# Row maxima of the 64-row attention heads from 128-row products

## The chip, the cores and the metric

The kernel runs on one core of a Trainium2 chip. The metric is the device time of one execution in microseconds (us); less is better. Before the change the median of three runs is 3290.38 us.

## What is computed

Two layers of a transformer over 512 image tokens and 256 context tokens, 1024 features wide. Each layer is a SwiGLU feed-forward network, a mixer and a second feed-forward network, each with a modulated norm ahead of it. The mixer projects its input, runs four mixers of four heads side by side and projects their outputs back. Cut to what matters here:

```
x  = x + 0.5*mx[2]*swiglu(pre_norm(x, ...))
ux = split_in(pre_norm(x, ...) @ w_in)
ya, yac = swa_mixer(...)        # windowed attention, 4 heads of 64, with a sink
yd, ydc = deltanet_mixer(...)   # gated delta rule, both directions
ym, ymc = mla_mixer(...)        # latent attention, 4 heads of 96 rows (64 + 32 rotary)
yn, ync = na_mixer(...)         # neighbourhood attention, 4 heads of 64, with a bias
x  = x + mx[5]*(concat([ya, yd, ym, yn]) @ w_out)
x  = x + 0.5*mx[8]*swiglu(pre_norm(x, ...))
...
def joint_softmax(*logits):     # local and context scores share one softmax
    p = softmax(concat(logits, axis=-1))
```

In the second layer only the image tokens are needed behind the mixer, so it has no context queries. Everything is float32 in the reference.

## The kernel before

The kernel is traced by a Tile scheduler: the code gives the operations in an order of its own, and the scheduler places them on the engines by its own estimate of their times, so that work of several generators is interleaved on each engine. Tiles of type F32R are single-pass products on TensorE; a float32 value is held as a pair of such tiles, high and low part, and a product takes three terms: high by high, low by high and high by low. Tiles of type F32 go through TensorE in a slower form (the values of the attention, the delta-rule chain, the transposes). Masks and biases are BF16.

The mixer stage of a layer has two generators side by side. `dn_chain` (lines 1193 to 1308) is the recurrence of the delta rule over 24 block steps, a chain of small products on TensorE (names t, mb, sp, op, pt, yt) with work of VectorE, ScalarE and GpSimd between them. `attentions` goes through twelve heads: four windowed ("swa"), four of the neighbourhood ("na"), four latent ("mla"). One step of the attention is traced for each step of the chain; when the chain ends, the rest of the attention follows. For each head and each block of 128 keys, `scores` makes transposed scores in PSUM (lines 687 to 689 for heads of 96 rows, 691 and 692 for heads of 64 rows, the mask on line 710), ScalarE takes the exponential (line 717, tile p), and `values` multiplies p by the values into tile o (lines 735 and 738). The next head's `row_max` runs beside these, up to four steps for each key block; two heads ahead, `load` issues the loads of queries and keys on GpSimd's queue.

`row_max` gives the number that is subtracted ahead of the exponential. For every block of 128 queries, line 637 multiplies the queries by the 256 context keys (tile sc) and line 644 by the image keys that the block sees (tile sl: 256 or 384 columns for a head of 64 rows, 512 for one of 96); lines 649 and 652 add masks and bias as further products into sl. VectorE reduces each with a maximum (lines 638 and 654). The sc and sl banks come from a PSUM ring of two, called r. At the end the maxima are transposed on TensorE (line 673, tile mt) and ScalarE writes them, negated, as one more row below the queries (line 674), where the score products pick them up against a row of ones in kb.

A head of 64 rows is loaded as these operands:

```
qa = [hi; hi] (128 rows)   qb = [lo; -max] (65 rows)
ka = [hi; lo] (128 rows)   kb = [hi; ones] (65 rows)
```

Line 691 multiplies ka by qa over 128 rows and line 692 kb by qb over 65. The row maxima come from `qh, kh = hd["q"][0], hd["k"][1]` (line 632), that is from qa and kb, cut to `Kd` rows: 64 for the swa and na heads, 96 for the mla heads. For the 64-row heads that is high by high alone.

The queues around it: `load_k` issues ka and then kb on GpSimd's queue, and `load_q` qa and then qb behind them. SyncE carries the weights, the stores of the mixers' outputs (yd) and their loads for the output projection (yl, line 1391). ScalarE carries the exponentials and, from the end of the chain on, casts of weights (wh) and of yl (xnhA, xnhC, line 269).

Of the kernel before, what the change touches and what calls it, by code (L numbers as in the profile page):

```python
# [6 lines left out]
F32 = mybir.dt.float32  # L7
# [5 lines left out]
PSUM = bass.MemoryType.PSUM  # L13

D = 1024
# [3 lines left out]
FF = 2816  # L19
# [14 lines left out]
class Net:  # L34
# [30 lines left out]
    def open_xn(self):  # L65
        """the normalised activations; their side of the memory changes with every opening"""
        self.side_x, self.side_o = self.side_o, self.side_x
        self.xnp = self.tc.tile_pool(name="xn", bufs=1, side=self.side_x, reuse_waits="tile")
        p = self.xnp.__enter__()
        self.XNh, self.XNl = {}, {}  # L70
        for q, t in self.T.items():
            self.XNh[q] = p.tile([128, KD, t], F32R, name="xnh" + q)
            self.XNl[q] = p.tile([128, KD, t], F32R, name="xnl" + q)
# [13 lines left out]
    def weights(self, pool, w, sets=None):  # L87
        """pool of the weight tiles. The raw tiles, free early, lie where the pool's successor puts its first tiles"""
        self.wp, self.ww, self.wsets, self.wn = pool, w, sets, -1
        tags = ["wr", "wh", "wl"] if sets is None else ["w%s%d" % (t, n) for n in range(sets) for t in "rhl"]  # L90
        left = self.side_x == "left"
        if sets is None:
            tags = tags if left else tags[1:] + tags[:1]
        else:
            tags = tags if left else tags[3:] + tags[:3]
        for t in tags:
            pool.tile([128, w], F32 if t[1] == "r" else F32R, tag=t, name=t)

    def psum(self, shape=(128, 512), name="pt", ring=None):
        """a PSUM bank of ring p, r or d; of self.rings in turn when none is named"""  # L100
        if ring is None:
            ring = self.rings[self.bank % len(self.rings)]
            self.bank += 1
        return self.ps.tile(list(shape), F32, tag=ring, name=name, bufs=BANKS[ring])

    def aux(self):
        """a ring of the attentions' side work: r, and d as well once the chain is traced"""
        self.auxn += 1
        return self.auxr[self.auxn % len(self.auxr)]

    # ---------------------------------------------------------------- inputs
# [5 lines left out]
    # ------------------------------------------------------- ada modulation  # L117
# [10 lines left out]
    def ada(self, l):  # L128
        """generator: modulation vectors of layer l, in steps of one weight row block.
        The first two vectors of layer 0 come from the tensor engine, the others are summed over the  # L130
        row blocks beside the FFNs, where it has no time to spare, and over the partitions at the end."""
# [15 lines left out]
        for j in range(2 if l == 0 else 0, 9):  # L147
            acc = [self.wa.tile([128, 512], F32, tag="acc", name="adaacc", bufs=AB) for _ in range(4)]
            for k in range(KD):
                for g in range(2):  # L150
                    w = self.wa.tile([128, 512], F32, tag="wa", name="adaw")
                    if l == 0 and j == 2 and k < WB // 2:
                        # no load before the first norm is done: its own come first
                        nc.gpsimd.tensor_copy(w[:, 0:1], self.XNl["A"][:, KD - 1, 0:1].bitcast(F32))
# [33 lines left out]
    def mod_cols(self, l, j):  # L188
        """scale -> g*(1+scale), gate of the sublayer (halved for the FFNs)."""
# [9 lines left out]
    def fill(self, n):  # L199
        """n steps of the work that is done beside the FFNs"""  # L200
# [4 lines left out]
    # ------------------------------------------------------------------ norm  # L205
    def unit(self, u):
        """A: the image's tokens, A0 and A1: halves of them, C: the context's; part, columns and their number"""
# [6 lines left out]
    def sumsq(self, u, m):  # L214
        """add chunk m of X to the running sum of squares."""
# [12 lines left out]
    def rstd_bc(self, ss, nb, dim, ring=None):  # L228
        """1/sqrt(sum(ss)/dim + eps) of every token, on all partitions."""
# [22 lines left out]
    def norm(self, u, i):  # L252
        """XN = X*rstd*g*(1+scale)+shift as an exact high/low pair."""
# [22 lines left out]
    # --------------------------------------------------------------- weights  # L276
    def weight(self, ap, w):
        """load a weight tile of w columns per partition, split into high/low."""
# [15 lines left out]
    # ------------------------------------------------------------------- FFN  # L294
    def ffn(self, l, i, parts, fill=0, save=(), then=None, ns=0):
        """X += gate * swiglu(XN); i-th sublayer's (0 or 2) modulation. then(unit): what follows a unit's last chunk"""
# [62 lines left out]
    # ---------------------------------------------------------------- output  # L359
    def final(self, u):  # L360
        """the final norm of a unit, to the output"""
# [11 lines left out]
def pack(inp):  # L373
# [14 lines left out]
    up = np.stack([np.stack([a[f"ffn{i}_wg"], a[f"ffn{i}_wu"]], 1) for i in (1, 2)], 1)  # L,2,2,D,FF  # L388
    r["wgu"] = c(up.reshape(L, 2, 2, KD, 128, NF, 128).transpose(0, 1, 5, 4, 2, 3, 6)).reshape(L, 2, NF, 128, 2, 1024)
    dn = np.stack([a["ffn1_wd"], a["ffn2_wd"]], 1)  # L,2,FF,D  # L390
# [8 lines left out]
class Mix:  # L399
    """projections of the mixers (kept in DRAM scratch ud) and the three attentions"""  # L400
# [27 lines left out]
    # ---------------------------------------------------------- projections  # L428
# [22 lines left out]
    def store(self, l, ch, parts, perm=False, fn=ACTF.Copy):  # L451
        """project chunk ch and keep it in ud"""
# [7 lines left out]
    def keep(self, ch, rows, w, src):  # L460
        """keep src, {first column: values}, as a high/low pair in hl or mk"""
# [6 lines left out]
        for j, t in enumerate((hi, lo)):  # L468
# [8 lines left out]
            else:  # L477
                # a head's rows: queries hi, hi, lo; keys hi, lo
# [4 lines left out]
    def store_pair(self, l, ch, parts, perm=False, rope=False):  # L483
        """project chunk ch and keep it as a high/low pair"""
# [15 lines left out]
    # ------------------------------------------------------ latent attention  # L500
    def mla_up(self, l, need):
        """normalised latents, their up-projections with the rotary part, to ud"""
# [37 lines left out]
        # shared rotary key: columns 32:64 of chunk 0, its swapped copy in 64:96; kept in rows 64:96  # L540
# [46 lines left out]
    # ------------------------------------------------------------ attention  # L587
    def load_v(self, ch):
        """values of the two heads of a chunk, token-major with a column of ones"""
# [12 lines left out]
    def load_q(self, ch, h, w):  # L602
        """a head of 64 rows as operands [hi; hi] and [lo]: with the keys' [hi; lo] and [hi] two products
        cover the three terms high*high, low*high and high*low"""
# [13 lines left out]
    def load_mla(self, h, w, kb):  # L618
        """a head of 96 rows as high/low pairs"""
# [8 lines left out]
    def row_max(self, hd):  # L628
        """minus the row maxima of the scores, in the row below the queries"""
        nc = self.nc  # L630
        Kd, nq, loc, bias = hd["Kd"], hd["nq"], hd["loc"], hd["bias"]
        qh, kh = hd["q"][0], hd["k"][1]
# [43 lines left out]
    def scores(self, hd, kb):  # L676
        """probabilities of the queries that see key block kb; kb None: the context's queries"""
# [42 lines left out]
    def values(self, hd, kb, pp):  # L720
        """add a key block's share to the unnormalised outputs, token-major; their column 64 sums the probabilities"""
# [3 lines left out]
        if kb == 4:  # L725
            # a product with zeros opens the bank for all blocks of queries
# [14 lines left out]
    def finish(self, hd):  # L741
        """normalise the outputs of a head; store them, feature-major, when both heads of a chunk are done"""
# [23 lines left out]
    def attentions(self, l, need):  # L766
# [5 lines left out]
        def edge(b):  # L772
            # the block on the left is masked where f < p, the one on the right where f > p
# [92 lines left out]
def mix_pack(inp, r):  # L866
# [9 lines left out]
    # rotary halves of the windowed heads: first halves of both axes, then second halves  # L876
# [4 lines left out]
    win = np.stack(chunks, 1)  # L,NCH,D,128  # L881
    r["win"] = c(win.reshape(L, NCH, KD, 128, 128).transpose(0, 1, 3, 2, 4)).reshape(L, NCH, 128, 1024)
    # rotary tables
# [22 lines left out]
    # masks  # L906
# [6 lines left out]
    def ok(qb, kb):  # [q, k]  # L913
# [25 lines left out]
    # latent attention  # L939
# [3 lines left out]
    uq = np.concatenate([uq, uq[:, :, :, 64:][:, :, :, sw]], 3)  # L,256,4,128  # L943
# [6 lines left out]
class DN:  # L950
    """gated delta rule mixer, both directions"""
# [14 lines left out]
    # -------------------------------------------------- projection and conv  # L966
    def dn_tokens(self, l, need, dp, dt):
        """short convolution and silu of k, q, v, token-major"""
# [28 lines left out]
    # -------------------------------------------------------------- gates  # L997
    def dn_gates(self, l, ab, gp, dt):
        """log decay g, beta [128 tok, 6, 8] and their cumulated forms"""
# [11 lines left out]
        # log1p(e) = 2 atanh(e / (2 + e))  # L1011
# [30 lines left out]
        egn = gp.tile([128, 2, 6, 2, 2], F32, name="egn")  # n, m, dir, pair  # L1042
# [7 lines left out]
    # ---------------------------------------------------------- preparation  # L1050
    def dn_prep(self, l, need, tok, ab, late, dp, dt):
        """normalised keys and queries, decays and the inverses of the 32x32 diagonal blocks"""
# [57 lines left out]
        def invert(d):  # L1110
# [11 lines left out]
            # 32x32 diagonal blocks, one block per partition, lower triangular  # L1122
# [29 lines left out]
    # ---------------------------------------------------------------- chain  # L1152
    def dn_chain(self, l, need, tok, prep, pc):
        """chunk-wise maps, state recurrence and outputs of both directions"""
# [18 lines left out]
        def chain(d):  # L1173
            for mi in range(6):
# [74 lines left out]
                # state recurrence and the outputs that depend on it  # L1249
# [42 lines left out]
    def dn_out(self, m, Oa, ng, pc):  # L1292
        """gated norm of a token block, feature-major, to the mixer outputs"""
# [43 lines left out]
class Kern(Net, Mix, DN):  # L1337
# [46 lines left out]
    def second_half(self, l, parts, then):  # L1384
        """output projection of the mixers and the second FFN"""
        nc = self.nc
        def take(k):
            for p in parts:
# [4 lines left out]
                if p == "A" and k >= 6:  # L1393
                    # the neighbourhood heads' blocks of columns, to the order of the tokens
# [16 lines left out]
        # the first output chunks, a mixer at a time in the order that they come  # L1411
# [40 lines left out]
    def mixers(self, l, need):  # L1452
# [13 lines left out]
        with ExitStack() as keep:  # L1466
# [4 lines left out]
            with ExitStack() as sx_st:  # L1471
                # a set of weight tiles after the other: the first lies on the raw tiles of the FFN's weights, which are free early
# [100 lines left out]
```

## Time and profile before

| what | us |
| --- | --- |
| timed runs | 3284.80, 3290.38, 3295.83 |
| median of the runs | 3290.38 |
| span of the profiled execution, first to last instruction | 3284.4 |
| stretch of the swa and na heads' maxima in layer 0 | 898 to 1065 |
| the same in layer 1 | 2615 to 2761 |

The profile has no run time of its own for the profiled execution, only its span; the median of the runs lies 6.0 us above that span. In a row of the timeline the second number is how long the instruction, or the run of like instructions, lasted; starts of successive products on TensorE are closer together than their durations, because products overlap in the array. In the chain of waits each piece is the time by which the end moved on, so that pieces add up to elapsed time. A form such as 64*128 64x256 is a product of 64 rows and 128 columns of weights with a moving operand of 256 columns. fp32r tiles are printed as f32.

### The profile page before, as it was taken

The numbers are of one execution on the slowest core, as the hardware profiler recorded it, in microseconds if no ns is written. First come the engines' busy times: TensorE is split into PE (matmuls) and PEld (weight loads), VectorE is DVE, ScalarE is ACT, GpSimd is POOL, SyncE is SP. The second block draws the span as 40 slices with busy tenths as digits, with TensorE's granted clock in tenths as the row PEclk, the third lists the DMA queues.
The fourth block names the chain that finished last, engine by engine and source line by source line (L and its number), as shares of the span: only waits on it lengthen the run. The fifth ranks groups of instructions, "written<-read, shape, count | busy, mean of one in ns | idle before, by whom it ended". The sixth has DMA issues, their size and how long they took to land.

```text
span 3284.4 us, 48913 instructions
## 1 busy us (share of the span) xinstructions
PE 3162.0 (96%) x19586; PEld 2721.2 (83%) x19586; DVE 1719.3 (52%) x3044; ACT 1069.4 (33%) x1927; POOL 465.6 (14%) x772
## 2 busy tenths in 40 slices
PE   7999999898999999999999999999997899999998
PEld 4888888887778889888889988888886688788887
DVE  5746354736744567766735432322747744353334
ACT  3212212555444423121224312122455343342223
POOL 2201000410323021111102000000311322000001
PEclk9999999998999999999999999999998999899999
DMA  6434232513623353444423221212423612323333
GB/s 246 148 103 140 83 118 81 170 59 119 175 71 81 90 193 114 157 134 136 134 73 117 67 68 58 71 52 66 147 77 113 169 49 70 118 92 98 95 96 107
DMA packets 135396, 357.45 MB, mean 109 GB/s; under 512 B 20000, under 2 KB 33824, under 8 KB 134912
## 3 DMA queue, kind: packets, MB, share of 16 engines
q1 hardware_dynamic: 101056, 255.47, 24.8%
q0 software_dynamic: 34112, 98.85, 10.6%
q8 instruction: 154, 2.52, 0.3%
q14 instruction: 74, 0.61, 0.1%
HBM read 316.89 MB, written 39.65 MB: 109 GB/s over the span
## 4 chain that ended last, share of the span: by engine, by line
PE 58%; DVE 3%; DMA 2%; ACT 1%; issue 1%; POOL 0%; SPq 0%; POOLq 0%; DVEq 0%; ACTq 0%
PE dacc L290 5%; PE dacc L291 5%; PE dacc L292 5%; PE gA L290 4%; PE gA L291 4%; PE uA L290 4%; PE uA L292 4%; PE uA L291 4%; PE gA L292 4%; PE guC L292 3%; PE guC L290 3%; PE guC L291 3%; PE o L738 2%; PE pj L292 1%; PE pj L290 1%
## 5 line engine op out<-in xcount | busy, mean ns | idle before, releaser
L269 ACT CAST wh<-wr 128x1024 fp32r<-128x1024 f32 (+5 forms) x443 | 394.8, 893 | 1235.2 <-PE dacc L291 454.8
L274 DVE TENSOR_TENSOR wl<-wr,wh 128x1024 fp32r<-128x1024 f32 (+5 forms) x443 | 460.6, 1042 | 420.0 <-ACT wh L269 390.4
L290 PE MATMUL dacc<-hh,wh 128*128 128x256 f32 (+1 forms) x1392 | 452.3, 326 | 2.6 <-ACT wh L269 2.3
L292 PE MATMUL dacc<-hh,wl 128*128 128x256 f32 (+1 forms) x1392 | 450.4, 326 | 2.8 <-DVE wl L274 2.8
L291 PE MATMUL dacc<-hl,wh 128*128 128x256 f32 (+1 forms) x1392 | 452.1, 326 | 0.0
L161 DVE SCALAR_TENSOR_TENSOR adaacc<-adaw,silc,adaacc 128x512 f32<-128x512 f32 x448 | 315.0, 747 | 11.4 <-DMA adaw<-ada_w 11.2
L290 PE MATMUL guC<-xnhC,wh 128*128 128x256 f32 x1056 | 300.4, 285 | 1.6 <-ACT xnhC L263 1.6
L291 PE MATMUL guC<-xnlC,wh 128*128 128x256 f32 x1056 | 300.3, 285 | 1.6 <-DVE xnlC L264 1.6
L292 PE MATMUL guC<-xnhC,wl 128*128 128x256 f32 x1056 | 300.2, 284 | 0.5 <-DVE wl L274 0.5
L290 PEld LDWEIGHTS dacc<-hh,wh 128*128 128x128 f32 x1392 | 261.4, 188 | 31.9 <-ACT wh L269 6.1
L290 PE MATMUL gA<-xnhA,wh 128*128 128x512 f32 (+1 forms) x752 | 285.3, 380 | 2.2 <-ACT xnhA L263 2.2
L292 PEld LDWEIGHTS dacc<-hh,wl 128*128 128x128 f32 x1392 | 261.0, 188 | 28.5 <-DVE wl L274 3.9
L290 PE MATMUL uA<-xnhA,wh 128*128 128x512 f32 (+1 forms) x752 | 283.1, 376 | 1.0 <-ACT wh L269 1.0
L292 PE MATMUL gA<-xnhA,wl 128*128 128x512 f32 (+1 forms) x752 | 283.4, 377 | 0.0
L292 PE MATMUL uA<-xnhA,wl 128*128 128x512 f32 (+1 forms) x752 | 282.8, 376 | 0.4 <-DVE wl L274 0.4
L291 PE MATMUL uA<-xnlA,wh 128*128 128x512 f32 (+1 forms) x752 | 283.0, 376 | 0.0
L291 PE MATMUL gA<-xnlA,wh 128*128 128x512 f32 (+1 forms) x752 | 282.9, 378 | 0.0
L291 PEld LDWEIGHTS dacc<-hl,wh 128*128 128x128 f32 x1392 | 261.4, 188 | 24.7
L133 POOL DMA_DIRECT2D adaw<-ada_w x256 | 140.1, 548 | 802.6 <-DVE adaacc L159 484.7
L348 DVE SCALAR_TENSOR_TENSOR xA<-dacc,modG,xA 128x512 f32<-128x512 f32 (+1 forms) x160 | 101.9, 640 | 239.3 <-PE dacc L292 239.3
L290 PEld LDWEIGHTS guC<-xnhC,wh 128*128 128x128 f32 x1056 | 203.1, 192 | 9.3 <-ACT wh L269 5.0
L291 PEld LDWEIGHTS guC<-xnlC,wh 128*128 128x128 f32 x1056 | 203.3, 193 | 4.4 <-DVE xnlC L264 2.0
(350 smaller groups left out, 5955.6 us busy)
## 6 DMA issues: line engine op xcount, KB each, us to landing
wr<-wgu SPq DMA_DIRECT2D x176, 512.0 KB, 3.6
adaw<-ada_w POOLq DMA_DIRECT2D x256, 256.0 KB, 3.2
wr<-wd SPq DMA_DIRECT2D x120, 320.0 KB, 3.0
wr<-wd SPq DMA_DIRECT2D x64, 384.0 KB, 3.1
wr<-win SPq DMA_DIRECT2D x44, 512.0 KB, 3.6
adaw<-ada_w SPq DMA_DIRECT2D x32, 256.0 KB, 5.2
hl<-eh SPq DMA_DIRECT2D x32, 192.0 KB, 3.0
hl<-el SPq DMA_DIRECT2D x24, 192.0 KB, 3.2
```

The lines of the kernel that those rows point to most:

```text
L133: load = lambda q, t, k, c: q.dma_start(out=t, in_=self.I["ada_w"][l, k * 128:(k + 1) * 128, c:c + 512])
L161: nc.vector.scalar_tensor_tensor(out=t, in0=w, scalar=c, in1=t, op0=ALU.mult, op1=ALU.add)
L269: nc.scalar.copy(hi, src)
L274: (nc.vector if leng == "V" else nc.gpsimd).tensor_tensor(lo, src, hi.bitcast(F32), op=ALU.subtract)
L290: nc.tensor.matmul(out, lhsT=wh, rhs=xh, start=start, stop=False)
L291: nc.tensor.matmul(out, lhsT=wh, rhs=xl, start=False, stop=False)
L292: nc.tensor.matmul(out, lhsT=wl, rhs=xh, start=False, stop=stop)
L348: nc.vector.scalar_tensor_tensor(out=x, in0=acc, scalar=gate[:, i, m, r:r + 1], in1=x, op0=ALU.mult, op1=ALU.add)
L738: nc.tensor.matmul(o[:, q0 + q], lhsT=p[:, q * 128:q * 128 + 128], rhs=v(kb), start=False, stop=kb == 3 and q == n // 128 - 1)
```

## The change

`row_max` takes, for heads with `Kd` of 64, all 128 rows: qa = [hi; hi] by ka = [hi; lo] in place of the upper 64 rows of qa by those of kb. The sum over 128 rows is high by high plus high by low. The latent heads keep their 96 rows and kb. No instruction is added or left out. Comments and docstrings are taken out elsewhere, which changes nothing; from here on lines are numbered two higher. The diff, cut to its core:

```diff
     def row_max(self, hd):
-        """minus the row maxima of the scores, in the row below the queries"""
+
         nc = self.nc
         Kd, nq, loc, bias = hd["Kd"], hd["nq"], hd["loc"], hd["bias"]
-        qh, kh = hd["q"][0], hd["k"][1]
+
+        Kd, kh = (128, hd["k"][0]) if Kd == 64 else (Kd, hd["k"][1])
+        qh = hd["q"][0]
         mx = self.tp.tile([128, 6, 2], F32, tag="mx", name="mx", bufs=2)
         for qb in range(nq):
             lq = qh[0:Kd, qb * 128:(qb + 1) * 128]
```

TensorE in layer 1, a neighbourhood head's maxima (L637, L644) among the scores (L691, L692), masks (L649, L710), bias (L652) and values (L738) of the head ahead of it, before:

```order
14197 L710 MATMUL st<-masks,identb 128x256
14198 L637 MATMUL sc<-kb,qa 128x256
14199 L738 MATMUL o<-v,p_25385 128x65 x4
14200 L691 MATMUL st<-qa,ka 128x384
14201 L692 MATMUL st<-qb,kb 128x384
14202 L644 MATMUL sl<-kb,qa 128x256
14203 L649 LDWEIGHTS identb
14204 L649 MATMUL sl<-masks,identb 128x256
```

And the same place after the change, its lines two higher:

```order
14193 L712 MATMUL st<-masks,identb 128x256
14194 L639 MATMUL sc<-ka,qa 128x256
14195 L740 MATMUL o<-v,p_25385 128x65 x4
14196 L693 MATMUL st<-qa,ka 128x384
14197 L694 MATMUL st<-qb,kb 128x384
14198 L646 MATMUL sl<-ka,qa 128x256
14199 L651 LDWEIGHTS identb
14200 L651 MATMUL sl<-masks,identb 128x256
```

Nothing has moved here; the two products of the maxima read ka where they read kb.

ScalarE in layer 0, where the latent heads (exponentials p, maxima mt) meet the output projection's casts (wh from weights, xnhA and xnhC from the loaded outputs yl), before:

```order
600 L674 ACTIVATE qa<-mt 1x512
601 L269 CAST wh<-wr 128x384 x2
602 L674 ACTIVATE qa<-mt 1x256
603 L269 CAST xnhA<-yl 128x512
604 L269 CAST xnhC<-yl 128x256
605 L717 ACTIVATE p_10550<-st 128x512
606 L717 ACTIVATE p_10570<-st 128x512
607 L269 CAST xnhA<-yl 128x512
608 L269 CAST xnhC<-yl 128x256
609 L717 ACTIVATE p_10598<-stc 128x512
610 L717 ACTIVATE p_10620<-st 128x512
```

After:

```order
600 L676 ACTIVATE qa<-mt 1x512
601 L269 CAST wh<-wr 128x384
602 L676 ACTIVATE qa<-mt 1x256
603 L269 CAST wh<-wr 128x384
604 L269 CAST xnhA<-yl 128x512
605 L719 ACTIVATE p_10550<-st 128x512
606 L269 CAST xnhC<-yl 128x256
607 L719 ACTIVATE p_10570<-st 128x512
608 L719 ACTIVATE p_10598<-stc 128x512
609 L269 CAST xnhA<-yl 128x512
610 L269 CAST xnhC<-yl 128x256
611 L719 ACTIVATE p_10620<-st 128x512
```

Three exponentials instead of two stand ahead of the second pair of casts, and one of the maxima's rows ahead of the second weight cast. Elsewhere the engines' orders differ in a few short runs, mostly in the same products of neighbouring work changing places.

## Rows read from the trace of the kernel before

**Rows 1.** The page's first line: the profiled execution.
```profile
span 3284.4 us, 48913 instructions
```

**Rows 2.** Groups by shape on TensorE: form, count | busy us, mean ns | idle before.
```profile
L637 PE MATMUL sc<-kb,qa 64*128 64x256 f32 x80 | 31.6, 396 | 3.3 <-DMA qa<-hl 3.1 <-DVE mx L638 0.2
...
L637 PE MATMUL sc<-kb,qa 96*128 96x256 f32 x40 | 15.7, 408 | 2.0 <-DVE mx L654 1.8 <-ACT v L599 0.2
...
L644 PE MATMUL sl<-kb,qa 64*128 64x384 f32 x32 | 14.1, 441 | 0.1
...
L644 PE MATMUL sl<-kb,qa 64*128 64x256 f32 x32 | 12.3, 385 | 0.2
```

**Rows 3.** Busy time in two stretches: PE, PEld, DVE, ACT, POOL; clock; DMA.
```profile
898.00:1065.00 167.00, 166.07 (x1441) 133.89 (x1440) 79.83 (x216) 72.03 (x184) 51.31 (x97) 1.00 0.35 79
2615.00:2761.00 146.00, 144.92 (x1220) 116.38 (x1221) 63.80 (x163) 61.18 (x157) 45.29 (x89) 0.95 0.30 78
```

**Rows 4.** TensorE's waits, 2615 to 2761 us: us in total, times, longest.
```profile
PE sc L637 <- DMA qa<-hl: 3.1, 1, 3.1
```

**Rows 5.** Timeline of TensorE in layer 1: start, duration, instruction, form.
```profile
2746.50 0.37 PE L691 MATMUL st<-qa,ka 128*128 128x256 f32 x1
2746.70 0.28 PE L692 MATMUL st<-qb,kb 65*128 65x256 f32 x1
...
2747.04 0.38 PE L637 MATMUL sc<-kb,qa 64*128 64x256 f32 x1
2747.35 1.11 PE L738 MATMUL o<-v,p 128*128 128x65 f32 x8
```

**Rows 6.** Chain of waits in the same place: start, us, what.
```profile
2746.75 0.12 PE st L691
...
2746.99 0.13 PE st L710
2747.11 0.31 PE sc L637
2747.42 1.04 PE o L738 x8
2748.46 0.23 PE st L691
...
2748.87 0.31 PE sl L644
2749.18 0.21 PE sl L649
...
2749.67 0.84 PE o L738 x8
```

**Rows 7.** Chain of waits among the latent heads of layer 0.
```profile
1135.62 0.84 PE o L735 x8
1136.46 0.17 PE sc L637
...
1137.80 0.12 PE sc L637
```

**Rows 8.** Timeline of TensorE, layer 1: maxima between chain products.
```profile
2750.66 0.33 PE L1264 MATMUL sp<-S,MT 64*64 64x64 f32 x4
2750.92 0.38 PE L637 MATMUL sc<-kb,qa 64*128 64x256 f32 x1
2751.23 0.33 PE L1264 MATMUL sp<-S,MT 64*64 64x64 f32 x4
```

**Rows 9.** Timeline, layer 1: a chain result and who reads it.
```profile
2662.18 0.69 DVE L1201 TENSOR_TENSOR vk<-vk,t 128x512 f32<-128x512 f32 x1 [0.24 <-PE t L1199]
...
2663.60 1.05 PE L1204 MATMUL t<-vk,tbd 128*128 128x128 f32 x8
```

**Rows 10.** Busy time as in rows 3, behind layer 0's last chain step.
```profile
1100.60:1103.60 3.00, 0.47 (x5) 0.23 (x3) 1.42 (x5) 0.17 (x1) 1.64 (x2) 1.00 0.41 97
1103.60:1118.40 14.80, 12.70 (x49) 9.46 (x49) 8.93 (x20) 6.47 (x13) 0.00 (x0) 0.54 0.62 194
```

## The prediction

> **What bounds the kernel now.** I first asked which engine sets the pace where the changed products stand. The profiled execution spans 3284.4 us [rows 1]; the three timed runs are 3284.80, 3290.38 and 3295.83, so their median lies 6.0 us above that span, and I carry the 6.0 us over. The changed products are those on lines 637 and 644 that run on 64 rows: 80 with 256 columns, and on line 644 32 with 256 and 32 with 384 columns, 144 in all; the 40 on line 637 that run on 96 rows belong to the latent heads and stay as they are [rows 2]. Along TensorE's timeline the 144 lie in two stretches, 898 to 1065 us (layer 0, 80 of them) and 2615 to 2761 us (layer 1, 64). The reader should see in the windows that TensorE is busy for 166.07 of 167.00 us and for 144.92 of 146.00 us there, while VectorE and ScalarE are busy for less than half of each [rows 3]. The one long wait, 3.1 us, is for a load of queries as the second stretch begins [rows 4]. In the chain of waits, followed back from the end, the second stretch is TensorE work laid end to end, and these very products are pieces of it [rows 6]. So TensorE's own sequence is the bound, and the question is what one 64-row product takes out of it, with what it does to its neighbours.
>
> **What a 64-row product costs today.** The timeline shows it. The 128-row L691 of 256 columns starts at 2746.50 and lasts 0.37, but the next product starts at 2746.70, 0.17 us before L691 is over: products overlap. The 64-row L637 starts at 2747.04 and lasts 0.38; the next product starts at 2747.35, only 0.07 us before its end [rows 5]. The next one, now of full height, has to get going anew. The chain of waits has the same as pieces that add up to the elapsed time: 0.31 us for the 64-row L637, 0.31 for the 64-row L644; the eight o products behind L637 take 1.04 us where eight behind a full-height product take 0.84; the mask product behind L644 takes 0.21, and a mask product of the same 256 columns behind a full-height product 0.13 [rows 6]. The two sorts of neighbour differ in nothing but the height of the product ahead.
>
> **What it will cost.** The change removes no instruction and adds none; it doubles the rows of both operands of 144 products. No row of before shows exactly the new product, but two are close. One is L637 itself for the latent heads, with 96 rows and 256 columns, the same kind of tiles, the same PSUM ring and the same reader: its piece is 0.17 us behind o products and 0.12 behind an fp32r product, and o products follow it and its like at 0.84 for eight [rows 7]. The other is L691, all 128 rows of the same ka and qa: 0.12 us for 256 columns behind a transpose, and 0.23 for 384 behind o products [rows 6]. So I take 0.17 behind o and mask products and 0.12 behind the others, which saves 0.14 or 0.19 of the 0.31. The 384-column ones cost 441 ns against 385 ns of busy time [rows 2], that is 56 ns for the further columns, which they will also cost in the new form; I give them the same savings.
>
> Who stands beside them is counted along TensorE's timeline of the two stretches. Ahead of the 144: 54 times an o or a mask product, 54 times another full-height product, 12 times another of the 144, and 24 times a product of the delta-rule chain that itself works on a part of the array. Behind them: 65 times a mask product, 34 times an fp32 product (o, a chain step, a transpose), 11 times an fp32r one, 12 times another of the 144, 22 times a chain product on a part of the array. Beside such partial products I count nothing: L1264 works on 64 by 64, and an L637 between two of them takes 0.31 us from start to start [rows 8]; the new form will still differ from both sides.
>
> The sum: own pieces 54 x 0.14 + 54 x 0.19 = 17.8 us; followers 65 x 0.08 (0.21 less 0.13) + 34 x 0.20 (1.04 less 0.84) + 11 x 0.19 (an fp32r follower, 0.31 less 0.12) = 14.1 us. Together 31.9 us. Bounds: if the new product takes 0.23 everywhere, the dearest ordinary piece of L691, and mask products gain nothing, it is 108 x 0.08 + 45 x 0.20 = 17.6 us; if all 108 save 0.19 and all 110 followers 0.20, it is 42.5 us. A loss from the products themselves I exclude, since every full-height piece of this size in these rows is under 0.31.
>
> **What moves with it.** Row maxima now wait for the load of ka rather than kb; the first score product, which reads both, waits for kb instead. Both loads leave GpSimd's queue together, and the queries leave it last: the only load that TensorE waits for there is that of qa [rows 4]. I cost this at nothing; if a ka load came late, the whole score sequence behind it would have waited for it anyway. No buffer is held longer, because the scores read ka after the maxima do. The order on the engines is almost the same. The larger differences stand where layer 0's latent heads meet the output projection: on ScalarE exponentials there move ahead of casts that wait for loads. I cost it at nothing, between plus and minus 2 us, since on either order TensorE has products queued.
>
> Is the gain passed on? What follows the stretches hangs on TensorE: the chain's steps, the stores of the mixers, and the loads that wait for those stores. The other engines' work stays as it is in stretches that shrink by a tenth, so VectorE's 79.83 of 167.00 us becomes about half. The chain's results lie ready before they are read: in the tightest case inside the stretches once the pipeline has filled, VectorE's L1201 ends at 2662.87 and L1204 reads it at 2663.60, 0.73 us later [rows 9]; it is the shortest of the 8 such pairs of the second stretch, the others have 1.34 us and more. Two shortened products within such a gap take some 0.6 us from it. So nearly all is passed on.
>
> **The rivals.** First, the height does not matter and the 0.31 us has another cause that stays (kb, the ring, the reductions): the time stays at 3290. Weighing against it: the 96-row products on the same line share kb, ring and reader and take 0.12 to 0.17 [rows 7]. The Trainium skill speaks for it, on the page TensorE: Matmul & The Clock Gate: under LDWEIGHTS (loading the stationary operand) the load's time goes by columns and not by the contraction, and the table under Why this matters for your kernels has a lone product of 32 rows take as long as one of 128. By that rule the change saves nothing; the trace agrees in busy time (385 and 396 ns for 64 rows, 408 ns for 96 [rows 2]) but not in when the neighbours start. I give it 6 in 100.
>
> Second, a partial gain: TensorE comes closer to its feeders and half of the 31.9 us goes into new waits for VectorE and ScalarE in the delta-rule chain, 3290.4 - 16 = 3274. For it: the 0.73 us of [rows 9]. Against: most gaps are several times that. 9 in 100.
>
> Third, slower: TensorE outruns the chain so far that it falls idle, and the granted clock falls. Such a place is in the trace, behind the last chain step of layer 0: 3.00 us with 0.47 busy, then 14.80 us at a granted clock of 0.54, close to 1.2 of 2.4 GHz [rows 10]. Its price is about 2.5 us idle and 14.8 x 0.46 = 6.8 us of slow products, 9.3 together. Four such stalls more would take the 31.9 us back; from five it is slower, at 3258 + 46 = 3304. It needs waits of microseconds where the gaps shrink by tenths: 3 in 100.
>
> **How the numbers follow.** The forecast is 3290.4 - 31.9 = 3258 us (span about 3252), with 82 in 100. Its own bounds are 3290.4 - 42.5 = 3248 and 3290.4 - 17.6 = 3273; with some 3 us of scatter, and the partial case mostly taken in, the range is 3245 to 3275. About 0.3%, 10 us, is what a measurement of this kernel can tell from no change, so faster means below 3280: the forecast, and nearly all of the partial case, 0.90. Within 0.3%: the first rival and the rest, 0.07. Slower: 0.03.
>
> **What would show it.** The groups of lines 637 and 644 (two lines lower in the new file) should drop from 385 and 396 ns on average towards 300 to 370, with 128 rows in their shape. The chain of waits should have 0.12 to 0.17 us where 0.31 stands, and eight o products behind them at 0.84. The first stretch should shrink by about 17 us and the second by about 14, with TensorE as busy as now. I am wrong if these pieces stay at 0.31; if they fall and the stretches do not shrink, the waits of TensorE on VectorE and ScalarE must have grown; if the stretches shrink and the end does not, a load or the clock in the tail of the attentions has taken it.

## The result, and the profile after

The changed kernel takes 3254.89 us (median of four runs, 3252.43 to 3255.82) against 3293.11 us for the kernel before beside it (3284.80 to 3299.08): a ratio of 0.9885, with a 95% interval from 0.9866 to 0.9904. It is faster by a little over 1%, 3 us below the forecast of 3258 and inside its range. The lines of the new file stand two higher: L637 is L639, L644 is L646, the scores' L691 is L693, the o products' L738 is L740.

The page's first line, and its row of engines, whose PE was 3162.0 us before:

```profile
span 3252.6 us, 48912 instructions
PE 3129.6 (96%) x19586; PEld 2713.3 (83%) x19586; DVE 1715.9 (53%) x3044; ACT 1069.6 (33%) x1927; POOL 463.6 (14%) x772
```

The span is 31.8 us shorter than in [rows 1], TensorE's busy time 32.4 us. VectorE's, ScalarE's and GpSimd's moved by 3.4 us at most. Groups by shape on TensorE, as in [rows 2] (form, count | busy us, mean ns | idle before):

```profile
L639 PE MATMUL sc<-ka,qa 128*128 128x256 f32 x80 | 30.0, 376 | 0.7 <-DVE mx L640 0.3 <-ACT v L599 0.3 <-ACT yt L764 0.2
...
L646 PE MATMUL sl<-ka,qa 128*128 128x384 f32 x32 | 13.2, 412 | 0.2
...
L646 PE MATMUL sl<-ka,qa 128*128 128x256 f32 x32 | 11.5, 359 | 0.4 <-DVE mx L656 0.3
```

The duration of one product fell by 20 to 29 ns, from 396, 441 and 385. Over 144 products that is 3.4 us, a tenth of the gain. Whoever reads the groups alone would take the change for nearly worthless. The gain stands in the places between the products. The chain of waits in layer 1, at the place of the work that answers to [rows 6] (start, us, what):

```profile
2712.14 0.12 PE st L693
...
2712.37 0.12 PE st L712
2712.50 0.12 PE sc L639
2712.62 0.84 PE o L740 x8
2713.46 0.23 PE st L693
...
2713.87 0.12 PE sl L646
2713.99 0.12 PE sl L651
...
2714.38 0.84 PE o L740 x8
...
2715.71 0.32 PE sc L639
2716.02 0.26 PE sp L1266 x4
```

Line by line against [rows 6]: the maxima product of line 639 has 0.12 us where 0.31 stood, the eight o products behind it 0.84 where 1.04 stood, line 646 has 0.12 for 0.31 and the mask product behind it 0.12 for 0.21. The last two rows are the place of [rows 8], between chain products on 64 by 64, and there the piece is 0.32 us still. TensorE's timeline of the same place (start, duration, instruction, form) answers to [rows 5]:

```profile
2712.26 0.37 PE L639 MATMUL sc<-ka,qa 128*128 128x256 f32 x1
2712.46 1.00 PE L740 MATMUL o<-v,p 128*128 128x65 f32 x8
```

The product itself lasts 0.37 us as against 0.38, but the next one now starts 0.17 us before its end and not 0.07. The weight loads (PEld, the loading of a product's stationary operand) of the same two rows, first before the change, then after:

```profile
2747.04 0.18 PEld L637 LDWEIGHTS sc<-kb,qa 64*128 64x128 f32 x1
2747.35 0.97 PEld L738 LDWEIGHTS o<-v,p 128*128 128x128 f32 x8
```

```profile
2712.22 0.20 PEld L639 LDWEIGHTS sc<-ka,qa 128*128 128x128 f32 x1
2712.34 0.98 PEld L740 LDWEIGHTS o<-v,p 128*128 128x128 f32 x8
```

The load of the o products followed 0.31 us behind that of the 64-row product and follows 0.12 us behind that of the 128-row one. Over the 144 products a load now starts a median of 55 ns behind the start of the product ahead, where it was 203 ns before; the load itself lasts about as long (192 and 183 ns). So the loads, which now run beside the product ahead, stood back until that product was nearly over.

The two stretches of [rows 3], cut at the same work (busy us of PE, PEld, DVE, ACT, POOL; clock; DMA):

```profile
895.00:1045.50 150.50, 149.01 (x1438) 129.67 (x1438) 78.07 (x214) 71.82 (x183) 52.81 (x99) 0.99 0.38 89
2595.00:2725.00 130.00, 129.39 (x1219) 112.81 (x1219) 62.78 (x163) 61.13 (x159) 44.34 (x87) 0.96 0.34 84
```

From first to last maxima product the first stretch went from 166.25 to 150.37 us and the second from 144.89 to 129.75. That is 15.9 and 15.1, together 31.0 of the 31.8 us, and TensorE is as full as before in both.

### The profile page after: what moved, and what is told of

Read it like the earlier page. It is cut to its first block, busy times and chain, and to the rows that moved or that the text cites. A ratio compares the mean times of both kernels' runs of the same rounds, so it can differ in the third digit from the quotient of the medians.

```text
span 3252.6 us, 48912 instructions
## 1 busy us (share of the span) xinstructions
PE 3129.6 (96%) x19586; PEld 2713.3 (83%) x19586; DVE 1715.9 (53%) x3044; ACT 1069.6 (33%) x1927; POOL 463.6 (14%) x772
## 4 chain that ended last, share of the span: by engine, by line
PE 57%; DVE 4%; issue 3%; DMA 2%; ACT 1%; POOL 0%; POOLq 0%; DVEq 0%; SPq 0%; ACTq 0%
PE dacc L290 4%; PE dacc L292 4%; PE dacc L291 4%; PE gA L290 4%; PE gA L291 4%; PE uA L290 4%; PE uA L292 4%; PE uA L291 4%; PE gA L292 4%; PE guC L292 3%; PE guC L290 3%; PE guC L291 3%; PE o L740 2%; PE pj L290 1%; PE pj L292 1%
```

## Experiments

Ratios are to the kernel before, run beside each, whose medians there lay between 3292.4 and 3294.9 us. The diffs are against the changed kernel where nothing else is said.

**The tile or the height.** The change swaps kb for ka as well as 64 rows for 128. This kernel takes the new tile and the old height; its order on every engine is that of the kernel before.

```
-        Kd, kh = (128, hd["k"][0]) if Kd == 64 else (Kd, hd["k"][1])
+        Kd, kh = (64, hd["k"][0]) if Kd == 64 else (Kd, hd["k"][1])
```

> The maxima of the 64-row heads from the upper 64 rows of qa and ka: the tile of the changed kernel with the height of the old one; the order on every engine is that of the kernel before. Height theory (a switch between products of at most 64 rows and taller ones costs TensorE the overlap on both sides): as before, ratio 1.00 within 0.3%, the span near 3284 us, 64-row pieces of 0.31 us in the chain of waits. Tile theory (kb, which holds the row of ones and is read by the last score product, is what made line 637 slow): the gain of the change, ratio 0.989.

3296.5 us, ratio 0.9999 (0.9975 to 1.0023). Nothing of the gain is left, so the tile and the wait that moved with it are worth nothing that this comparison can tell (its interval is 8 us to either side). Its chain of waits in layer 1:

```profile
2743.05 1.03 PE o L740 x8
2744.09 0.31 PE sc L639
2744.40 0.12 PE sl L646
2744.52 0.22 PE sl L651
```

Here two 64-row products follow each other. The first has 0.31 us, the second 0.12, and the mask product behind the pair 0.22 again. It is not being low that costs, but the passage from tall to low and back.

**One row more than 64.** The same, with 65 rows; the order is again that of the kernel before.

```
-        Kd, kh = (128, hd["k"][0]) if Kd == 64 else (Kd, hd["k"][1])
+        Kd, kh = (65, hd["k"][0]) if Kd == 64 else (Kd, hd["k"][1])
```

> One row more than the last: 65 rows of qa and ka (the sum is high by high plus one row of high by low, so the maxima are a little different from both kernels'), same order on every engine as the kernel before. Height theory with a border at 64: the whole gain, 32 us by the sum of the prediction, ratio 0.990 (0.9885 as measured for 128 rows). If the gain grew with the number of rows: 1/64 of it, ratio 0.9998. If a part of the gain of the change came from its changed order on the engines, this one is slower than the changed kernel by that part; the height theory has them equal within 0.3%.

3266.8 us, ratio 0.9905 (0.9876 to 0.9934). A single row brings most of the gain. Its chain of waits at the place of [rows 6], and a product between o products:

```profile
2707.65 0.17 PE o L740 x2
2707.82 0.17 PE sc L639
2707.99 0.17 PE o L740 x2
...
2720.06 0.12 PE st L712
2720.19 0.12 PE sc L639
2720.31 0.84 PE o L740 x8
...
2721.55 0.12 PE sl L646
2721.67 0.13 PE sl L651
```

These are the pieces of the 128-row product. Added up as under The sum below, the 144 products take 29.0 us and their followers 17.1, against 28.7 and 16.8 in the kernel after and 46.3 and 30.9 in the kernel before. The border therefore lies between 64 and 65 rows, and 65 behaves as 128 does. The Trainium skill has a rule that fits, on the page TensorEngine Tiling (Array Packing), in the section Tiling Modes: row tiles have 32, 64 or 128 rows, and a change of tiling mode drains TensorE. It gives no price; here it is 0.14 to 0.19 us on the product and 0.09 to 0.20 on its follower. No run here shows in which mode a 64-row product is issued.

**More rows still.** 120 rows have the order of the kernel before, 127 rows that of the kernel after; each replaces the 128 in the same line.

> 120 rows of qa and ka for the maxima of the 64-row heads (eight rows of high by low left out of the sum), which leaves the order on every engine as in the kernel before and in the 65-row one. Height theory: as 65 rows, ratio 0.990. If more rows than 65 bring more: as the changed kernel, 0.987. If the order of before costs the 6 to 12 us by which the 65-row kernel stood behind the changed one: as 65 rows, and behind the 127-row kernel by that much.

> 127 rows (one row of high by low left out), which gives the order of the changed kernel on every engine. Height theory: as the changed kernel, ratio 0.987 to 0.9885. Order theory: ahead of the 120-row kernel by 6 to 12 us with the granted clock 0.977 to 0.979 over the run against 0.971 to 0.976; no order effect: the two within 0.3% of each other, 10 us, and nearer than that on average.

3256.2 us, ratio 0.9859 (0.9816 to 0.9903), and 3255.7 us, 0.9855 (0.9807 to 0.9902). The order that the change moves is worth 0.6 us, within the scatter. The kernel after, run once more beside other kernels:

> The changed kernel once more, on the same chip as the 65-row one and in as many rounds. Height theory: ratio 0.988 to 0.990, and the same as 65 rows within 0.3%. If the changed order on the engines matters: apart from the 65-row kernel by more than that.

3254.5 us, ratio 0.9873 (0.9845 to 0.9901). The 65-row kernel's median stands some 10 us above that of the 120-row one. Yet the two profiled executions, both at a mean granted clock of 0.973, span 3259.2 and 3260.1 us, so at this clock the two are alike. The runs of the 65-row kernel had a lower clock more often (0.971 to 0.976, against 0.973 to 0.976), which may be all of the 10 us; the runs are too few to say so.

**Each product twice.** What does a second product behind the first cost? First the kernel before with every 64-row maxima product issued twice, then the kernel after with every 128-row one so. The excerpt shows line 637 in the first; line 644 is changed in the same way.

```
+            if Kd == 64:
+                nc.tensor.matmul(sc, lhsT=lq, rhs=kh[0:Kd, TX:768])
             nc.tensor.matmul(sc, lhsT=lq, rhs=kh[0:Kd, TX:768])
```

> The kernel before with each of the 144 64-row products issued twice in a row into the same bank (144 products more, 112 of 256 and 32 of 384 columns). Height theory: the second of a pair needs no switch and costs what a full-height product costs behind its like, 112 x 0.12 + 32 x 0.18 = 19 us more, ratio 1.006. If a 64-row product is slow by itself: 112 x 0.31 + 32 x 0.37 = 47 us more, ratio 1.014.

> The changed kernel with each of the 144 128-row products issued twice in a row. Every theory: 19 us more than the changed kernel (112 x 0.12 + 32 x 0.18), that is 3274, ratio 0.994 to the kernel before. It measures a product's own price, beside which the same repetition of the 64-row products shows whether these are dearer by themselves.

3314.3 us, ratio 1.0057 (1.0037 to 1.0076), and 3269.2 us, 0.9901 (0.9872 to 0.9930): by the medians 19 us more than the kernel before and 15 more than the kernel after (by the ratios 19, and 5 to 9). The traces are sharper: the second products' pieces add up to 20.1 us with 64 rows and to 19.2 with 128, where 19 was expected of both. If each 64-row product carried its 0.31 us within itself, 144 more would have cost some 45 us. The pairs in the chain of waits of the first of the two:

```profile
2729.51 0.31 PE sc L638
2729.82 0.12 PE sc L639
2729.93 1.09 PE t L1236 x8
2731.02 0.31 PE sl L647
2731.34 0.12 PE sl L648
2731.45 0.22 PE sl L653
```

First 0.31, then 0.12, and the dear follower stands behind the second. A passage with two low products in it cost the same as a passage with one.

**One line at a time.** Only line 637's products on 128 rows, then only line 644's. The excerpt is that of the first, which puts line 644 back on 64 rows of kb.

```
-            nc.tensor.matmul(sl, lhsT=lq, rhs=kh[0:Kd, k0 * 128:k1 * 128], start=True, stop=loc is None)
+            Ks, ks = (64, hd["k"][1]) if Kd == 128 else (Kd, kh)
+            nc.tensor.matmul(sl, lhsT=qh[0:Ks, qb * 128:(qb + 1) * 128], rhs=ks[0:Ks, k0 * 128:k1 * 128], start=True, stop=loc is None)
```

> One part alone: the 80 products over the context keys (line 637) on 128 rows, the 64 over the image keys (line 644) on 64 rows of kb as before; order on every engine as before. Height theory: own pieces and followers summed for these alone give 17.1 us, 3273, ratio 0.995.

> The other part alone: the 64 products of line 644 on 128 rows, the 80 of line 637 on 64 rows of kb. Height theory: 11.0 us, 3279, ratio 0.9966. The two parts together make 28.1 of 31.9 us, since 12 products stand directly behind another of the 144 and a switch between the two is left in either part. If gains were lost to other waits as they add up, the two parts would make more than the whole.

3276.0 us, ratio 0.9928 (0.9895 to 0.9961), and 3280.3 us, 0.9945 (0.9921 to 0.9970): 18 to 24 us for the 80 and 14 to 18 for the 64, as one counts from the medians or from the ratios. The parts add up to the whole as closely as these runs can tell (ratios 0.72% and 0.55% below one, together 1.27%, against 1.15 and 1.27% for the kernel after in its two comparisons, each part with an interval of 0.25 to 0.33% to either side).

**Low products put in elsewhere.** The other direction: the kernel after, with one further product ahead of each of the 72 maxima products of the latent heads, which have 96 rows. It goes into the same bank and is overwritten. The excerpt shows line 637; line 644 is changed in the same way. Once it has 64 rows, once 65; the two kernels have the same order on every engine.

```
+            if Kd == 96:
+                nc.tensor.matmul(sc, lhsT=lq[0:64], rhs=kh[0:64, TX:768])
             nc.tensor.matmul(sc, lhsT=lq, rhs=kh[0:Kd, TX:768])
```

> The suspected cost added elsewhere: the changed kernel, and ahead of each of the 72 96-row products of the latent heads' maxima a 64-row product of the same columns into the same bank, which the 96-row one then overwrites. Height theory: each 64-row product takes 0.31 us where a like one takes 0.12, and the 96-row one behind it 0.31 in place of 0.12 to 0.17: 40 x 0.47 + 32 x 0.57 = 37 us more than the changed kernel, 3292, ratio 1.00 to the kernel before. If height does not matter: 40 x 0.12 + 32 x 0.23 = 12 us more, 3267, ratio 0.992.

> The twin of the kernel with 64-row products ahead of the latent heads' maxima: these 72 further products have 65 rows, all else and the order on every engine are the same. Height theory: 12 us more than the changed kernel, 3267, ratio 0.992, and the granted clock, which stayed at half for 102 us in the 64-row twin while TensorE was busy throughout, is back at full some 15 us after the wait at the end of the delta-rule chain. If the further products or the changed order made the 64-row twin slow (3343): the same here, ratio 1.01, and the same 102 us at half clock.

3342.9 us, ratio 1.0116 (1.0076 to 1.0157), and 3301.7 us, 0.9999 (0.9967 to 1.0030). The 64 rows cost 41 us more than the 65, in the direction expected, but both lie far above their forecasts of 3292 and 3267. The windows of the 64-row kernel, then of the 65-row one, show why (columns as above; the clock is the last but two):

```profile
1095.00:1105.00 10.00, 9.37 (x22) 5.03 (x22) 6.33 (x14) 5.51 (x11) 0.00 (x0) 0.50 0.72 225
1105.00:1140.00 35.00, 35.00 (x111) 26.22 (x110) 10.01 (x22) 9.44 (x18) 0.00 (x0) 0.50 0.16 46
```

```profile
1095.00:1105.00 10.00, 8.47 (x31) 6.27 (x31) 6.28 (x15) 5.38 (x11) 0.00 (x0) 0.50 0.74 236
1105.00:1140.00 35.00, 35.00 (x136) 31.48 (x136) 11.58 (x25) 9.27 (x19) 0.00 (x0) 0.50 0.12 34
```

TensorE is busy for 35.00 of 35.00 us, and the granted clock is 0.50, that is 1.2 of 2.4 GHz. In the trace it stays there from 1090.3 to 1192.7 us and from 2827.7 to 2892.5 with 64 rows, and from 1088.8 to 1180.9 and 2812.5 to 2850.0 with 65. In the kernel after the half clock at this place (1084.3 to 1098.0 us) ends after 13.7 us. In all three it fell where the chain ends and TensorE has to wait: of the two microseconds from 1088 to 1090 it was busy for 1.13 in the 64-row kernel. So these two kernels measure two things at once. Their profiled spans differ by 34.6 us; within them they spent 271.2 and 231.3 us at half clock in all, and half of that difference, an estimate of its price, is 20 us. Some 15 us are left for the height of 72 products, where 25 were expected. Against the profiled span of the kernel after, with 151.0 us at half clock, the 65-row kernel has 47.2 us more, of which half of 80.3 us go to the clock and 7 are left for the products; the 64-row kernel has 81.8 us more, 60 for the clock and 22 for the products. By the same estimate the products thus cost less than the 12 and 37 us expected.

**A further product of the same height.** Is it the further products that hold the clock down, or that they are lower than their neighbours? The same kernel with 96 rows, the height of the product that follows.

```
+            if Kd == 96:
+                nc.tensor.matmul(sc, lhsT=lq[0:96], rhs=kh[0:96, TX:768])
```

> The kernel after, with a further product ahead of each of the 72 row-maxima products of the latent heads, as in the twins with 64 and with 65 rows, but here of 96 rows, the height of the product that follows it into the same bank and overwrites it. It tells apart what the long stretch at half clock of the two twins (1088 to 1193 us and 2812 to 2893 us, with TensorE busy throughout) goes with. By the theory that a further product of another height than its neighbours brings it (mixed heights), the stretches are short again here, as in the kernel after (some 14 us each), and the time is that of the kernel after plus 72 pieces of 0.12 to 0.23 us: 3255 + 9 to 17 = 3264 to 3272. By the theory that the further products at this place bring it, whatever their height, the stretches stay some 90 and 38 us long, and the time is that of the twin with 65 rows, 3295 to 3305. The order of the instructions differs from that of the twins in places, which the twins' comparison with each other did not have.

3258.1 us, ratio 0.9893 (0.9857 to 0.9929): 3 to 4 us above the kernel after. The same windows:

```profile
1095.00:1105.00 10.00, 10.00 (x48) 8.54 (x47) 6.34 (x13) 5.29 (x12) 0.00 (x0) 0.68 0.47 140
1105.00:1140.00 35.00, 35.00 (x259) 32.22 (x259) 12.20 (x29) 16.03 (x31) 0.00 (x0) 1.00 0.15 46
```

The clock is back at 1101.5 us, 17 us after it fell, and TensorE gets through 259 products in the 35 us instead of 136 or 111. The timed runs agree with the profiles: their mean granted clock is 0.977 to 0.982 here, 0.958 to 0.959 with 64 rows and 0.963 to 0.970 with 65. That further products at this place hold the clock down whatever their height has fallen. That it goes with the lower height, 64 or 65 rows among 96, is not shown: the order of the instructions differs here in places from that of the other two, and no run parts the two. Two readings of the traces speak against height as the whole of it. The last further product of layer 0 is issued at 1158.7 us with 64 rows and at 1145.7 with 65, yet the clock is back only 34 and 35 us later. And stretches of 34 to 44 us at half clock stand in kernels without such products as well: 2632.1 to 2676.5 us in the 64-row kernel on ka, 2774.8 to 2808.9 in the 65-row one, 2828.7 to 2862.8 in the one with each 64-row product twice. The time lies below the expected 3264 to 3272; the profiled execution spent 131.5 us at half clock against 151.0 in the kernel after, and half of that difference, by the same estimate 10 us, would fill the gap.

## Why the prediction was right

**What bounds the kernel.** Right. TensorE's own sequence was the bound in both stretches, it is as full as before, and what was taken from it reached the end: 31.0 us in the stretches, 31.8 in the span.

**What a 64-row product costs.** Right in size, and now with its cause. The step said that the product loses its overlap at both sides. The pairs show that this belongs to the change of height, not to the low product: the second of two has 0.12 us. The weight loads show where the time goes: the low product's load and that of its follower stand back until the product ahead is nearly over. The first rival, that height does not matter, fell with the 64-row kernel on tile ka and the 65-row kernel. The rule it came from is that of the Trainium skill, page TensorE: Matmul & The Clock Gate, section Why this matters for your kernels, by which a lone product of few rows takes as long as one of 128. The trace bears it out for the duration (376 to 396 ns at either height) and not for products among others, where the measurement decides: 0.31 us against 0.12 to 0.17.

**The sum.** I added up, over the 144 products of both traces, the time from the end of the product ahead to the end of the product, and from there to the end of the one behind (ends are modelled, and waits over 0.7 us are left out). Own pieces went from 46.3 to 28.7 us, 17.6 saved against 17.8 forecast. Followers, without the 12 that are themselves of the 144, went from 30.9 to 16.8, 14.1 saved against 14.1. The single terms hold as well: 65 mask products went from a median of 0.214 to 0.125 us (0.09 each, forecast 0.08), and 15 o products from 0.254 to 0.057 (0.20, forecast 0.20). Own pieces behind o and mask products saved 0.146 each, against 0.14. Leaving out the neighbours on a part of the array was right too: their places kept 0.31 to 0.32 us as product and 0.197 as follower.

**What was mis-sized.** The 6.0 us by which the median stood above the profiled span, which I carried over. After the change it is 2.3 us (3254.9 less 3252.6), and that is the 3 us by which the forecast lies too high. Runs whose span is on record take 1.7 to 1.8 us longer than it; the rest of the 6.0 was the spread of the kernel before, whose profiled execution was one of its faster ones. So the sum is borne out by the spans (3252.6 us against about 3252), while the medians lie 38 us apart, 6 more than the sum. That is within the interval of the ratio, which makes the gain 32 to 44 us, but the prediction had no term for it, and that the time was still met within 3 us is in part luck. The part of the first stretch was put at 17 us and that of the second at 14; they were 15.9 and 15.1. The groups' means were to fall to between 300 and 370 ns, and line 639's came to 376; the mean has four products at half clock in it, and without them it is 366.

**The moved order and the moved wait** were costed at nothing, within 2 us. The pair of 120 and 127 rows gives 0.6 us for the order, and the 64-row kernel on ka gives nothing for the wait.

**The rivals of waits and clock.** In the two stretches TensorE's waits after the change are 1.0 and 0.6 us in all, so the partial gain did not come. The fall of the clock did not come with this change either: both profiled executions have about the same time at half clock, 156.2 us before and 151.0 after. The further low products show that the price was real, and that no more stalls were needed for it: the clock fell at the wait that was there before, and then stayed at half for 102 and 92 us with TensorE busy for 101.6 and 90.3 of them. The rival, which had the clock back some 15 us after each stall, was too narrow.

## What to carry to other kernels

Read the cost of a small matmul from start to start, or from the chain of waits, and not from its duration: here group means that fell by 5 to 7% hid pieces that fell by half. Where a product on 64 rows stands among taller ones on a busy TensorE, look for a way to give it more than 64, by stacking operands that are loaded anyway, or put such products next to each other, so that several share one passage. Before a time is put down to such products, look at the granted clock of the stretch: in two of the experiments here it took more than their height did.

## What the runs showed of the hardware

The border is sharp: 64 rows against 65, on the same tile and in the same order, gave 3296.5 and 3266.8 us.

The granted clock can stay at half for 102 us while the profile has TensorE busy for 101.6 of them, as it did with the 64-row products among the 96-row ones; the last 31.7 us of this (1161.0 to 1192.7) came behind all of the 64-row products, with TensorE busy for 31.7. The Trainium skill has the clock return when TensorE is busy (page TensorE: Matmul & The Clock Gate, section Part 1: The HAM clock gate (the "warmup" mystery)). These two runs do not agree with that, if busy is what the profile calls busy; the run with 96 rows does, with 17 us at half clock.

The spread of the kernel before goes with the clock as well. The ten runs of the 64-row kernel on ka, which has the same order, lie nearly in the order of their mean granted clock, from 3286.5 us at 0.977 to 3325.8 at 0.963, while those of the kernel after lie between 0.976 and 0.979. So the medians differ by 38 to 40 us where the two profiled executions differ by 31.8. That low products bring the lower clock is not shown: the profile of the 120-row kernel, too, has 23.9 us at half clock among the maxima (963.8 to 987.7), where that of the kernel after has none between 896.6 and 1084.3. What brings such stretches stays open.
